# Latent attention on one core: the order of its pieces laid down for TensorE alone, one preparation transpose per q tile, projections further ahead, rotary k scaled by POOL

## The chip, the cores and the metric

The kernel runs on one core of a Trainium2 chip, as one program launch. The metric is device time in microseconds (us), from the start to the end of an execution; lower is better. TensorE (PE in the profile) multiplies matrices, VectorE (DVE), ScalarE (ACT) and GpSimd (POOL) work element by element, and SyncE (SP) issues the transfers between HBM and the core's on-chip memory.

## What is computed

Two layers on a residual stream x of 512 rows by 2048 columns, in float32. Layer A is a gated pooling mixer; then one shared key/value side is made, and layer B is a latent attention of 16 heads. Only the attention matters here; the reference, cut to it:

```python
def chunk_causal_attention(q, k, v):
    S = q.shape[1]
    scale = QK_HEAD ** -0.5
    outs = []
    for i in range(S // QBLOCK):
        q0, k_end = i * QBLOCK, (i + 1) * QBLOCK
        s = jnp.einsum('bqhd,bkhd->bhqk', q[:, q0:k_end], k[:, :k_end]) * scale
        q_chunk = (q0 + jnp.arange(QBLOCK)) // CHUNK
        k_chunk = jnp.arange(k_end) // CHUNK
        s = jnp.where((k_chunk[None, :] <= q_chunk[:, None])[None, None], s, -1e30)
        p = jax.nn.softmax(s, axis=-1).astype(v.dtype)
        outs.append(jnp.einsum('bhqk,bkhd->bqhd', p, v[:, :k_end]))
    return jnp.concatenate(outs, axis=1)

def mla_layer(x, k, v, norm_g, w_in, q_latent_g, w_q_b, q_norm_g, w_out, cos, sin):
    ...
    q = (rmsnorm(q_lat, q_latent_g) @ w_q_b).reshape(B, S, N_HEADS, QK_HEAD)
    q = qk_norm_rope(q, q_norm_g, cos, sin)
    o = chunk_causal_attention(q, k, v).reshape(B, S, W_B)
    return x + (o * jax.nn.silu(gate)) @ w_out
```

k and v of a head come from a latent of 512 columns by `kv_w_b`; k has 128 columns of its own and 64 rotary columns that all heads share, and is normed like q. The kernel computes every product in three passes (high by high, high by low, low by high part), so every operand is split in two: ACT casts the high part, DVE subtracts it to get the low part.

## The kernel before

The program has three stages on TensorE. The first two (layer A and the projections into latents and gates) are dense runs of matmuls up to about 1440 us. The third is the attention with the output projection, up to the end.

**Groups, heads, tiles.** The 16 heads go in 8 groups (`hg`) of two heads (`h`), each head in 4 q tiles (`i`). A group's 8 tiles are numbered 0 to 7 here (4h + i).

**Preparation of a group** (`prep_items`). `kv_part` (L641 to L643) projects k and v of both heads, 4 row tiles of 4 pieces, each piece three matmuls of 512 columns; `q_part` (L664 to L666) does so for q, with 384 columns. A piece reads one of four weights, loaded by SP into `raw`, cast by ACT (L126, `whi`) and subtracted by DVE (L127, `wlo`); four of them are held, and the next is loaded when the weight four before it has had its last use. `kstats_unit` forms the inverse norm of k on DVE: sums of squares from ACT, L684 and L685, a reciprocal square root of three Newton steps (L158 to L163) on tiles of 128x8, and then eight scalings of k in place (L692). `krot_unit` scales the shared rotary k by it, once for each head (L700, on ACT). `qstats_unit` does the same for q, whose factor goes into the exponential; `qrot_unit` (L721 to L724, on POOL) rotates q. At last `tr_unit` transposes what the scores read, through a PSUM bank `tr`: units 0 and 1 are k of the two heads, unit 2 the rotary k of a head (L736), units 3 and 4 q of the two heads, and unit 5 the rotary q (the others at L753). Four TensorE transposes of 128x128 make a unit; ACT and DVE then read the bank to split it.

**A tile of attention.** `score_unit` multiplies q by k (L787, five matmuls of up to 512 columns) into one of two `sc` banks; DVE masks (L788), takes the row maximum (L790) and multiplies it by the norm of q (L792). `exp_unit` lets ACT form the exponential with its sum (L800). `scale_unit` takes the reciprocal (L806) and scales (L807) on DVE. `pt_unit` transposes P on TensorE (L815), through the same two `tr` banks, and splits it (L149, the line of the helper `split`). `pv_unit` multiplies by v (L840 to L842) after every second tile, and at a head's end DVE multiplies by the gate (L845).

**What sets the order.** The main loop walks over the 64 tiles: score of tile m, PV of m-2 where due, exponential of m, transpose of P of m-1, scaling of m. Between these it calls `fill_to`, which takes pieces from one long list, `fill`: the preparation of all groups, two gates, the first parts of the output projection. Each entry has a length in TensorE time, and `base` says how much of the list must be done when a group's first tile begins: up to its last preparation transpose (unit 5) and 2.3 us more (`AHEAD`). At the end the instructions of this stage are chained on TensorE, ACT and DVE, each in the order in which the program wrote them; POOL and SP are left to the scheduler, which orders an engine's instructions by its own plan. TensorE, ACT, DVE and POOL each work through their queue in order, so an instruction that waits holds up all behind it.

Of the kernel before, what the change touches and what calls it, by code (L numbers as in the profile page):

```python
# [10 lines left out]
AF = mybir.ActivationFunctionType  # L11
ALU = mybir.AluOpType
AX = mybir.AxisListType

P = 128
# [25 lines left out]

AHEAD = 2.3


@with_exitstack
def trunk_kernel(
# [17 lines left out]
    V, A, G, T = nc.vector, nc.scalar, nc.gpsimd, nc.tensor  # L66
# [21 lines left out]
    def tt_(n=S, dt=F32):  # L88
        return tp[0].tile([P, n], dt, tag="t", name="tt_")
# [10 lines left out]
    def f(ap):  # L100
        return ap.bitcast(F32)
# [46 lines left out]
    def split(src, hi, lo):  # L148
        return A.copy(hi, src), V.tensor_tensor(lo, src, f(hi), ALU.subtract)  # L149
# [112 lines left out]
    with ExitStack() as c1:  # L262
# [97 lines left out]
        with ExitStack() as c2:  # L360
            hp = c2.enter_context(tc.tile_pool(name="hp", bufs=2, **tile_))
            for j in range(NJ):
# [3 lines left out]
                c = x_load(j)  # L366
                raw = hp.tile([P, 4, 2, P], F32, tag="hraw", name="hraw")
                hi = w7.tile([P, 4, 2, P], F32R, tag="hi", name="hi")
                lo = w7.tile([P, 4, 2, P], F32R, tag="lo", name="lo")
                parts = None  # L370
                for m in (0, 2):
# [3 lines left out]
                    parts = parts or x_parts(j, c, hp)  # L375
# [16 lines left out]
        for o in range(0, 4, 2):  # L392
            e = epool.tile([P, 7, H], F32, tag="e", name="e")
# [72 lines left out]
    for g in range(NG):  # L466
# [11 lines left out]
        for o in range(KD):  # L478
            first = len(wloads)
# [15 lines left out]
    for k in range(KD):  # L495
        hi, lo = at(), at()
# [182 lines left out]
    def kstats_unit(hg):  # L679

        d = st[hg]
        v, a, y = small(8, "sv", 2), small(8, "sa", 2), small(8, "sy", 2)
        for t in range(4):
            V.tensor_scalar(v[:, 2 * t:2 * t + 2], d["ssk"][:, 2 * t:2 * t + 2], kr2[:, t:t + 1], None, ALU.add)  # L684
        V.tensor_scalar(v, v, 1.0 / 192, EPS, ALU.mult, ALU.add)  # L685
        rsqrt(v, y, a, 8)
        d["yk"] = y
        for t in range(4):
            for h in range(2):
                c = 2 * t + h  # L690
                kk = d["kraw"][t // 2][:, t % 2, h * P:(h + 1) * P]
                V.tensor_scalar(kk, kk, y[:, c:c + 1], None, ALU.mult)  # L692

    def krot_unit(hg, h):
        d = st[hg]
        y = d["yk"]
        d.setdefault("krs", []).append(tt_())
        for t in range(4):
            c = 2 * t + h
            A.activation(d["krs"][h][:, t * P:(t + 1) * P].rearrange("p (a d) -> p a d", a=2),  # L700
                         krr[:, t:t + 1, :].broadcast_to([P, 2, 64]), AF.Copy, scale=y[:, c:c + 1])

    def qstats_unit(hg):

# [66 lines left out]
    def score_unit(hg, h, i):  # L771
        d = st[hg]
        n = (i + 1) * P
        if i == 2:

            gt = d[("G", h)] = bt(dt=F32)
            nc.sync.dma_start(gt, gates[2 * hg + h])
        s = sc()
        kh, kl = d[("T", h)]
        krh, krl = d["kr"][h]  # L780
        qh, ql_ = d[("T", 3 + h)]
        qr = d["qr"][h]
# [5 lines left out]
        V.memset(s[0:64, n - 64:n], -1e30)  # L788
        nm = small(1, "nm", 4)
        V.tensor_reduce(nm, s[:, 0:n], AX.X, ALU.max)  # L790
        rq = d["rq"][:, 2 * i + h:2 * i + h + 1]
        V.scalar_tensor_tensor(nm, nm, -1.0, rq, ALU.mult, ALU.mult)  # L792
        d[("P", h, i)] = s, nm, rq
# [9 lines left out]
    def scale_unit(hg, h, i):  # L803
        pe, sm = st[hg][("P", h, i)]
        n = (i + 1) * P
        V.reciprocal(sm, sm)  # L806
        V.tensor_scalar(pe[:, 0:n], pe[:, 0:n], sm, None, ALU.mult)  # L807

    def pt_unit(hg, h, i):

        d = st[hg]
        pe, _ = d.pop(("P", h, i))
        p = tr()
        for j in range(i + 1):
            T.transpose(p[:, j * P:(j + 1) * P], pe[:, j * P:(j + 1) * P], ident)  # L815
# [4 lines left out]
        c = (i % 2) * P  # L820
        for a in range((i + 2) // 2):
            nb = min(2, i + 1 - 2 * a)
            src = p[:, 2 * a * P:(2 * a + nb) * P].rearrange("p (j q) -> p j q", j=nb)
            split(src, d["pth"][a][:, 0:nb, c:c + P], d["ptl"][a][:, 0:nb, c:c + P])

    def pv_unit(hg, h, pr):
        d = st[hg]
# [22 lines left out]
    def prep_items(hg, nxt, mid=()):  # L850


        def piece(us, fn, *a, w=None):
            return us, w, fn, a

        def k(t, i):
            return piece(0.69, kv_part, hg, t, i, w=(wkvb[hg, :, i * 512:(i + 1) * 512], 512))

        def q(t, i):
            return piece(0.53, q_part, hg, t, i, w=(wqb[hg, :, i * 384:(i + 1) * 384], 384))  # L860

# [10 lines left out]
        end = hg == nhg - 1  # L872
        first += mid
        if end:
            first += ld(0, 1, 2, 3)
        first += [q(0, 0), q(0, 1), kq(3), q(0, 2), q(0, 3), piece(0, kstats_unit, hg),
                  q(1, 0), q(1, 1), qq(0), q(1, 2), q(1, 3), kr(0), tr_(0), qq(1), tr_(1),
                  q(2, 0), q(2, 1), kr(1)] + (og(0) if end else []) + [
                  q(2, 2), tr_(2, 0), q(2, 3), tr_(2, 1)] + (og(1) + ld(4, 5) if end else []) + [
                  q(3, 0), qq(2), q(3, 1)] + (og(2) + ld(6, 7) if end else []) + [  # L880
                  q(3, 2), q(3, 3)] + (og(3) if end else [])
        return (first + nxt[:2] + [qq(3), piece(0, qstats_unit, hg), tr_(3)] + nxt[2:3] + [tr_(4)] +
                nxt[3:4] + [tr_(5)] + nxt[4:])


    ogs = [None] * NH
# [121 lines left out]
    base, c = [], 0.0  # L1008
    for t, _, fn, a in fill:
        c += t  # L1010
        if fn is tr_unit and a[1] == 5:
            base.append(c + AHEAD)
    base.append(c)
    SLOT, MAIN = 12.2 / 8, (0.99, 2.0, 1.09, 2.03)
    fill_to(base[0])
    seq = [(hg, h, i) for hg in range(nhg) for h in range(2) for i in range(4)]


    for m in range(len(seq) + 2):
        now = seq[m] if m < len(seq) else None  # L1020
        if now:
            hg, h, i = now
            each = (base[hg + 1] - base[hg]) / 8
            at_ = base[hg] + each * (4 * h + i) + sum(SLOT - MAIN[j] for j in range(i))
            share = each + SLOT - MAIN[i]
            score_unit(*now)
        if m >= 2 and seq[m - 2][2] % 2:
# [92 lines left out]
```

## Time and profile before

| what | us |
|---|---|
| three runs | 2058.01, 2057.32, 2051.13 |
| their median | 2057.32 |
| the profiled execution | 2057.44 |
| its span, first to last instruction | 2055.7 |
| first matmul of the first `kv_part` | 1439.9 |
| first score of group 0 | 1499.82 |
| first score of group 7 | 1863.56 |

The span is the time between the first and the last instruction on the core; the execution's own time is 1.74 us longer. In the slices of the page, each 51.4 us long, the attention fills numbers 30 to 37 of 40. A digit there is the busy share of an engine in tenths; PEclk is the clock that TensorE was granted, in tenths of full speed. In a row of groups the columns are line, engine, operation, output<-inputs, shape and count, then busy us and mean ns, then the idle time ahead of it and what ended it. In a row of waits: who waited for whom, us in total, times, the longest. In the timeline: start, length, instruction, and in brackets the wait before it with what ended it.

### The profile page before, as it was taken

How to read it: one execution, taken by the hardware profiler on the slowest of the kernel's cores; microseconds unless marked ns; L12 is line 12 of the kernel's file. 1: busy time of each engine (PE TensorE's matmuls, PEld its weight loads, DVE VectorE, ACT ScalarE, POOL GpSimd, SP SyncE). 2: the span in 40 equal slices, each digit the busy share in tenths (PEclk: the TensorE clock that was granted, in tenths of full speed). 3: DMA queues.
4: the chain of work that ended last, by engine and by line, in shares of the span. 5: the costliest groups of instructions: out<-in, count | busy, mean ns of one | idle time of the engine just before them, and what ended most of it. 6: DMA issues, size and time to landing. Idle time of an engine off the chain costs nothing. (4 is left out here: it accounts for less than half of the span.)

```text
span 2055.7 us, 30705 instructions
## 1 busy us (share of the span) xinstructions
PE 1961.6 (95%) x11356; PEld 1735.4 (84%) x11356; DVE 1300.5 (63%) x2297; ACT 828.0 (40%) x1570; POOL 253.0 (12%) x404
## 2 busy tenths in 40 slices
PE   8999999999999999999999999999977888888999
PEld 7999999999999778888888888888866777777887
DVE  8677776886666774866845666533466666666432
ACT  7434333333334332333334533322455555554221
POOL 0423333332231000000000000000111111110000
PEclk9999999999999999999999999999989888889999
DMA  5544444344444464344433433334221111222642
GB/s 186 167 154 155 144 134 128 124 140 144 134 148 146 152 199 131 123 138 123 139 118 121 147 97 103 113 118 123 89 67 57 57 57 57 65 89 85 207 123 88
DMA packets 176647, 251.27 MB, mean 122 GB/s; under 512 B 15728, under 2 KB 95984, under 8 KB 176496
## 3 DMA queue, kind: packets, MB, share of 16 engines
q1 hardware_dynamic: 176208, 249.10, 38.6%
q8 instruction: 89, 1.46, 0.3%
q14 instruction: 62, 0.51, 0.1%
q10 hardware_dynamic: 288, 0.20, 0.0%
HBM read 216.21 MB, written 33.03 MB: 121 GB/s over the span
## 5 line engine op out<-in xcount | busy, mean ns | idle before, releaser
L126 ACT CAST whi<-raw 128x512 fp32r<-128x512 f32 (+2 forms) x421 | 254.0, 608 | 521.6 <-PE mm L145 432.4
L333 PE MATMUL k<-xc,hi 128*128 128x256 f32 x1680 | 460.1, 283 | 0.1
L335 PE MATMUL k<-xc,hi 128*128 128x256 f32 x1680 | 460.0, 283 | 0.0
L127 DVE TENSOR_TENSOR wlo<-raw,whi 128x512 fp32r<-128x512 f32 (+2 forms) x421 | 283.1, 674 | 262.3 <-ACT whi L126 258.0
L337 PE MATMUL k<-xc,lo 128*128 128x256 f32 x1680 | 417.9, 283 | 1.4 <-DVE lo L315 1.3
L144 PE MATMUL mm<-bt,whi 128*128 128x512 f32 x944 | 368.2, 390 | 2.8 <-ACT bt L149 2.8
L146 PE MATMUL mm<-bt,wlo 128*128 128x512 f32 x944 | 368.7, 391 | 1.5 <-DVE wlo L127 1.5
L145 PE MATMUL mm<-bt,whi 128*128 128x512 f32 x944 | 367.7, 390 | 0.1
L315 DVE TENSOR_TENSOR lo<-raw,hi 128x1792 fp32r<-128x1792 f32 x120 | 249.0, 2075 | 158.3 <-ACT hi L314 158.2
L314 ACT CAST hi<-raw 128x1792 fp32r<-128x1792 f32 x120 | 202.7, 1689 | 362.9 <-PE k L337 253.3
L333 PEld LDWEIGHTS k<-xc,hi 128*128 128x128 f32 x1680 | 322.5, 192 | 0.4 <-ACT hi L314 0.3
L335 PEld LDWEIGHTS k<-xc,hi 128*128 128x128 f32 x1680 | 322.5, 192 | 0.0
L337 PEld LDWEIGHTS k<-xc,lo 128*128 128x128 f32 x1680 | 296.8, 192 | 2.7 <-DVE lo L315 2.2
L144 PEld LDWEIGHTS mm<-bt,whi 128*128 128x128 f32 x944 | 177.3, 188 | 40.6 <-ACT bt L149 3.7
L146 PEld LDWEIGHTS mm<-bt,wlo 128*128 128x128 f32 x944 | 177.3, 188 | 39.7 <-DVE wlo L127 2.7
L145 PEld LDWEIGHTS mm<-bt,whi 128*128 128x128 f32 x944 | 177.3, 188 | 37.5 <-DVE bt L149 0.9
L146 PE MATMUL mm<-at,wlo 128*128 128x512 f32 x432 | 169.1, 391 | 1.4 <-DVE wlo L127 1.4
L145 PE MATMUL mm<-at,whi 128*128 128x512 f32 x432 | 169.7, 393 | 0.3 <-DVE at L149 0.2
L144 PE MATMUL mm<-at,whi 128*128 128x512 f32 x432 | 169.2, 392 | 0.0
L310 POOL TENSOR_TENSOR raw<-raw 128x256 f32<-128x256 f32 x120 | 98.5, 821 | 439.8 <-DVE raw L308 423.3
L311 POOL TENSOR_TENSOR raw<-raw 128x256 f32<-128x256 f32 x120 | 98.9, 824 | 9.2
L146 PEld LDWEIGHTS mm<-at,wlo 128*128 128x128 f32 x432 | 81.5, 189 | 19.3 <-DVE wlo L127 2.3
(1150 smaller groups left out, 2608.7 us busy)
## 6 DMA issues: line engine op xcount, KB each, us to landing
raw<-awin SPq DMA_DIRECT2D x240, 256.0 KB, 3.2
raw<-awo SPq DMA_DIRECT2D x128, 256.0 KB, 2.8
raw<-bwin SPq DMA_DIRECT2D x80, 256.0 KB, 2.8
raw<-awg SPq DMA_DIRECT2D x64, 256.0 KB, 2.8
raw<-bwo SPq DMA_DIRECT2D x59, 256.0 KB, 2.8
scr<-e SPq DMA_DIRECT2D x56, 256.0 KB, 2.6
raw<-wkvb SPq DMA_DIRECT2D x32, 256.0 KB, 2.9
raw<-wqb SPq DMA_DIRECT2D x32, 192.0 KB, 2.4
```

Of the source, the lines that this page charges most:

```text
L126: A.copy(hi[:, :n], raw[:, :n])
L127: V.tensor_tensor(lo[:, :n], raw[:, :n], f(hi[:, :n]), ALU.subtract)
L144: T.matmul(dst, wh, xh, start=first, stop=False)
L145: T.matmul(dst, wh, xl, start=False, stop=False)
L146: T.matmul(dst, wl, xh, start=False, stop=last)
L310: G.tensor_tensor(c[:, :, 6, :], c[:, :, 4, :], c[:, :, 2, :], ALU.add)
L311: G.tensor_tensor(c[:, :, 7, :], c[:, :, 6, :], c[:, :, 3, :], ALU.add)
L314: A.copy(hi, c[:, :, 1:8, :])
L315: V.tensor_tensor(lo, c[:, :, 1:8, :], f(hi), ALU.subtract)
L333: T.matmul(dst, hi[:, j % 2, wi, :], xh[j][:, xi, :], start=first, stop=False, skip_group_check=True)
L335: T.matmul(dst, hi[:, j % 2, wi, :], xl[j][:, xi, :], start=False, stop=False, skip_group_check=True)
L337: T.matmul(dst, lo[:, j % 2, wi, :], xh[j][:, xi, :], start=False, stop=last, skip_group_check=True)
```

## The change

The diff, cut to its core:

```diff
-AHEAD = 2.3
+AHEAD = 6.5
...
     def kstats_unit(hg):
...
-        for t in range(4):
-            for h in range(2):
-                c = 2 * t + h
-                kk = d["kraw"][t // 2][:, t % 2, h * P:(h + 1) * P]
-                V.tensor_scalar(kk, kk, y[:, c:c + 1], None, ALU.mult)
+        for a in range(2):
+            kk = d["kraw"][a].rearrange("p b (h c) -> p (b h) c", h=2)
+            V.tensor_tensor(kk, kk, y[:, 4 * a:4 * a + 4].unsqueeze(2).broadcast_to([P, 4, P]), ALU.mult)

     def krot_unit(hg, h):
...
-        for t in range(4):
-            c = 2 * t + h
-            A.activation(d["krs"][h][:, t * P:(t + 1) * P].rearrange("p (a d) -> p a d", a=2),
-                         krr[:, t:t + 1, :].broadcast_to([P, 2, 64]), AF.Copy, scale=y[:, c:c + 1])
+        o = tt_()
+        yk = d["yk"].rearrange("p (t h) -> p t h", h=2)[:, :, h:h + 1].broadcast_to([P, 4, 64])
+        ov = o.rearrange("p (t a d) -> p t a d", t=4, a=2)
+        for a in range(2):
+            G.tensor_tensor(ov[:, :, a, :], krr, yk, ALU.mult)
+        d.setdefault("krs", []).append(o)
...
     def pt_unit(hg, h, i):
...
-            split(src, d["pth"][a][:, 0:nb, c:c + P], d["ptl"][a][:, 0:nb, c:c + P])
+        for src, hi, lo in parts:
+            A.copy(hi, src)
+        for src, hi, lo in parts:
+            V.tensor_tensor(lo, src, f(hi), ALU.subtract)
...
-        if fn is tr_unit and a[1] == 5:
+        if fn is q_squares and a[1] == 3:
             base.append(c + AHEAD)
     base.append(c)
-    SLOT, MAIN = 12.2 / 8, (0.99, 2.0, 1.09, 2.03)
+    MAIN = (0.99 + 0.45, 2.0 + 0.45, 1.09 + 0.45, 2.03)
+    SLOT = sum(MAIN) / 4
...
+    side = {(0, 1): [(0, tr_unit, 1)], (1, 1): [(0, tr_unit, 2, 1)], (2, 1): [(0, tr_unit, 4), (1, kstats_unit)],
+            (3, 1): [(1, krot_unit, 0)], (4, 1): [(1, tr_unit, 0), (1, krot_unit, 1)], (5, 1): [(1, tr_unit, 2, 0)],
+            (6, 1): [(1, qstats_unit), (1, tr_unit, 3)], (7, 0): [(1, tr_unit, 5)]}
...
             scale_unit(*now)
+            beside(hg, 4 * h + i, 1)
             fill_to(at_ + share)
     fill_to(c + 99)
+    PINNED = (mybir.EngineType.PE,)
     prev = {}
     for ins in block[begin:]:
         e = ins.engine
-        if e in (mybir.EngineType.PE, mybir.EngineType.Activation, mybir.EngineType.DVE):
+        if e in PINNED:
```

In `side` the key is a tile of the group and the half of the tile; the entries are what is written there, with 0 for the group itself and 1 for the next one. So of a group's seven transposes those of its second head (units 1, 2 and 4) move into its own tiles 0 to 2, and the others into tiles 4 to 7 of the group before; the statistics of k come in tile 2 of the group before, those of q in tile 6. In `prep_items` these pieces leave the list, except in group 0, which keeps units 0, 2 (head 0), 3 and 5 and its statistics there. `base` now counts up to the last squares of q, and 6.5 us more. ACT and DVE are no longer chained. A helper's line stands no longer for the split of P, which the change writes out (L826 and L828), and the lines behind the first edit shift: L752 and L735 are the preparation transposes, L786 the scores, L814 the transpose of P, L787, L789, L791, L805 and L806 the DVE steps of a tile, L690 the scaling of k.

**TensorE, between the last tile of head 0 and the second of head 1, in a middle group.** Names: `tt__` is a scaled tile P, `tr` the bank, `mm` a projection piece, `sc` a score; x8 means eight alike in a row. Before:

```order
L815 MATMUL tr<-cs,tt__16485 128x128 x3
L664 MATMUL mm<-whi,at 128x384
L665 MATMUL mm<-whi,at 128x384
L666 MATMUL mm<-wlo,at 128x384
L753 MATMUL tr<-cs,at 128x128 x8
L787 MATMUL sc<-bt 128x128 x5
```

Now, from the first score of head 1 on (of the four pieces of `mm` around the transposes one is shown):

```order
L786 MATMUL sc<-bt 128x128 x5
L814 MATMUL tr<-cs,tt__16534 128x128 x4
L664 MATMUL mm<-whi,at 128x384
L665 MATMUL mm<-whi,at 128x384
L666 MATMUL mm<-wlo,at 128x384
L752 MATMUL tr<-cs,at 128x128 x4
L786 MATMUL sc<-bt 128x256 x5
```

The two units of k stood back to back ahead of head 1's first score; now one unit stands in head 1's first tile, behind the transpose of P and projection pieces, and the other has moved into the next group.

**DVE, the statistics of k, in a middle group.** `sv`, `sa` and `sy` are the 128x8 tiles of the square root, `kr` the rotary part of the norm, `at` holds k. Before (the second and third Newton step, alike, are left out):

```order
L807 TENSOR_SCALAR tt__16485<-tt__16485,sm 128x384
L684 TENSOR_SCALAR sv<-ssk,kr_12522 128x2 x4
L685 TENSOR_SCALAR sv<-sv 128x8
L158 TENSOR_SCALAR sy<-sv 128x8
L159 TENSOR_SCALAR sv<-sv 128x8
L161 TENSOR_TENSOR sa<-sy 128x8
L162 TENSOR_TENSOR sa<-sa,sv 128x8
L163 SCALAR_TENSOR_TENSOR sy<-sa,sy 128x8
L692 TENSOR_SCALAR at<-at,sy 128x128 x8
L788 MEMSET sc 64x64
L790 TENSOR_REDUCE nm<-sc 128x1
```

Now, from a Newton step on:

```order
L161 TENSOR_TENSOR sa<-sy 128x8
L805 RECIPROCAL sm<-sm 128x1
L162 TENSOR_TENSOR sa<-sa,sv 128x8
L806 TENSOR_SCALAR tt__17011<-tt__17011,sm 128x384
L163 SCALAR_TENSOR_TENSOR sy<-sa,sy 128x8
L765 SCALAR_TENSOR_TENSOR bt<-tr,gqk,bt 128x512
L787 MEMSET sc 64x64
L789 TENSOR_REDUCE nm<-sc 128x1
L791 SCALAR_TENSOR_TENSOR nm<-nm,qy 128x1
L690 TENSOR_TENSOR at<-at,sy 128x512 x2
```

The statistics were one unbroken block ahead of the next tile's mask; now a tile's reciprocal, scaling, mask and maximum lie between their steps.

**DVE, behind the maximum of head 1's second tile.** `nm` is the maximum, `wlo` a weight's low part, `ov` the result of PV. Before:

```order
L788 MEMSET sc 64x64
L790 TENSOR_REDUCE nm<-sc 128x1
L792 SCALAR_TENSOR_TENSOR nm<-nm,qy 128x1
L845 TENSOR_TENSOR bt<-ov,bt 128x512
L127 TENSOR_TENSOR wlo<-raw,whi 128x512 x2
```

Now (a third `wlo`, alike, stands between L849 and L791):

```order
L787 MEMSET sc 64x64
L127 TENSOR_TENSOR wlo<-raw,whi 128x512
L789 TENSOR_REDUCE nm<-sc 128x1
L149 TENSOR_TENSOR bt<-tr,bt 128x512
L849 TENSOR_TENSOR bt<-ov,bt 128x512
L791 SCALAR_TENSOR_TENSOR nm<-nm,qy 128x1
```

The product behind the maximum followed it at once; now an eviction, the gate's product and a weight's low part stand between the two.

More of the change, by code (lines that the diff above doesn't have):

```diff
@@ L820, in pt_unit @@
         c = (i % 2) * P
+        parts = []
         for a in range((i + 2) // 2):
             nb = min(2, i + 1 - 2 * a)
-            src = p[:, 2 * a * P:(2 * a + nb) * P].rearrange("p (j q) -> p j q", j=nb)
-            split(src, d["pth"][a][:, 0:nb, c:c + P], d["ptl"][a][:, 0:nb, c:c + P])
+            parts.append((p[:, 2 * a * P:(2 * a + nb) * P].rearrange("p (j q) -> p j q", j=nb),
+                          d["pth"][a][:, 0:nb, c:c + P], d["ptl"][a][:, 0:nb, c:c + P]))
+        for src, hi, lo in parts:
+            A.copy(hi, src)
+        for src, hi, lo in parts:
+            V.tensor_tensor(lo, src, f(hi), ALU.subtract)
     def pv_unit(hg, h, pr):
@@ L872, in prep_items @@
         end = hg == nhg - 1
+        own = hg == 0
         first += mid
@@ L875, in prep_items @@
             first += ld(0, 1, 2, 3)
[L876 to L883, printed above, removed]
+        first += [q(0, 0), q(0, 1), kq(3), q(0, 2), q(0, 3)]
+        if own:
+            first += [piece(0, kstats_unit, hg)]
+        first += [q(1, 0), q(1, 1), qq(0), q(1, 2), q(1, 3)]
+        if own:
+            first += [kr(0), tr_(0)]
+        first += [q(2, 0), qq(1), q(2, 1)]
+        if own:
+            first += [kr(1)]
+        if end:
+            first += og(0)
+        first += [q(2, 2), q(2, 3)]
+        if own:
+            first += [tr_(2, 0)]
+        if end:
+            first += og(1) + ld(4, 5)
+        first += [q(3, 0), qq(2), q(3, 1)]
+        if end:
+            first += og(2) + ld(6, 7)
+        first += [q(3, 2), q(3, 3)]
+        if end:
+            first += og(3)
+        first += nxt[:1] + [qq(3)]
+        if own:
+            return first + [piece(0, qstats_unit, hg), tr_(3)] + nxt[1:4] + [tr_(5)] + nxt[4:]
+        return first + nxt[1:]
     ogs = [None] * NH
@@ L1010, in trunk_kernel, with beside @@
         c += t
-        if fn is tr_unit and a[1] == 5:
+        if fn is q_squares and a[1] == 3:
             base.append(c + AHEAD)
     base.append(c)
-    SLOT, MAIN = 12.2 / 8, (0.99, 2.0, 1.09, 2.03)
+    MAIN = (0.99 + 0.45, 2.0 + 0.45, 1.09 + 0.45, 2.03)
+    SLOT = sum(MAIN) / 4
     fill_to(base[0])
     seq = [(hg, h, i) for hg in range(nhg) for h in range(2) for i in range(4)]
+    side = {(0, 1): [(0, tr_unit, 1)], (1, 1): [(0, tr_unit, 2, 1)], (2, 1): [(0, tr_unit, 4), (1, kstats_unit)],
+            (3, 1): [(1, krot_unit, 0)], (4, 1): [(1, tr_unit, 0), (1, krot_unit, 1)], (5, 1): [(1, tr_unit, 2, 0)],
+            (6, 1): [(1, qstats_unit), (1, tr_unit, 3)], (7, 0): [(1, tr_unit, 5)]}
+    def beside(hg, n, part):
+        for x, fn, *a in side.get((n, part), ()):
+            if hg + x < nhg:
+                fn(hg + x, *a)
     for m in range(len(seq) + 2):
@@ L1026, in trunk_kernel @@
             score_unit(*now)
+            beside(hg, 4 * h + i, 0)
         if m >= 2 and seq[m - 2][2] % 2:
```

2 lines of the change are left out of this document (removed).

## The prediction

> **What bounds the kernel now.** I read the page first. TensorE is busy nearly all the time except in slices 32 to 37, which are the attention; there the granted clock drops too.
>
> ```profile
> PE 1961.6 (95%) x11356; PEld 1735.4 (84%) x11356; DVE 1300.5 (63%) x2297; ACT 828.0 (40%) x1570; POOL 253.0 (12%) x404
> PE   8999999999999999999999999999977888888999
> PEclk9999999999999999999999999999989888889999
> ```
>
> Then the table by stretches, cut at the first score matmul of a group of two heads (1499.82 us is group 0, 1863.56 group 7; the third row is group 3, typical of the middle). Columns: length, then busy time of PE, PEld, DVE, ACT, POOL, then granted clock.
>
> ```profile
> 1475.00:1499.82 24.82, 20.13 (x88) 16.54 (x88) 15.60 (x51) 14.99 (x47) 6.78 (x16) 0.82 0.21 66
> 1499.82:1863.56 363.74, 294.84 (x1540) 253.63 (x1539) 242.03 (x778) 206.07 (x673) 45.50 (x112) 0.88 0.21 66
> 1654.01:1705.23 51.22, 41.76 (x221) 36.10 (x220) 34.11 (x111) 28.89 (x97) 6.45 (x16) 0.87 0.18 57
> 1863.56:1905.00 41.44, 36.66 (x190) 30.41 (x189) 26.02 (x72) 18.76 (x48) 0.00 (x0) 0.96 0.21 65
> ```
>
> In the seven groups TensorE idles 363.74 - 294.84 = 68.9 us, and the clock takes (1 - 0.88) x 363.74 = 43.6 us more at most (some of the half-speed time falls into the waits). So TensorE's own work at full clock is at least 294.84 - 43.6 = 251.2 us, or 35.1 us in group 3 (41.76 - 0.13 x 51.22), against 51.2 us taken. No other engine is full: DVE 67%, ACT 57%.
>
> Next, whom TensorE waits for in the attention (us in total, times, longest).
>
> ```profile
> PE tr L753 <- DVE xt L149: 19.5, 6, 3.3
> PE tr L753 <- DVE bt L766: 18.5, 7, 2.7
> PE tr L753 <- DVE at L692: 15.8, 7, 2.5
> PE tr L815 <- DVE sc L788: 6.7, 10, 1.8
> PE tr L736 <- DVE xt L149: 5.5, 6, 0.9
> ```
>
> The preparation transposes (L753, L736) carry 19.5 + 18.5 + 15.8 + 5.5 = 59.3 us. The timeline shows how one such pair arises in group 3:
>
> ```profile
> 1669.55 1.12 DVE L684 TENSOR_SCALAR sv<-ssk,kr 128x2 f32<-128x2 f32 x4
> ...
> 1672.93 0.17 DVE L163 SCALAR_TENSOR_TENSOR sy<-sa,sy 128x8 f32<-128x8 f32 x1
> 1673.14 1.66 DVE L692 TENSOR_SCALAR at<-at,sy 128x128 f32<-128x128 f32 x8
> 1673.57 1.41 PE L753 MATMUL tr<-cs,at 128*128 128x128 f32 x4 [2.24 <-DVE at L692]
> 1674.80 0.11 DVE L788 MEMSET sc<- 64x64 f32 x1
> ...
> 1675.86 0.78 ACT L800 ACTIVATE tt__16571<-sc,nm,qy 128x512 f32<-128x512 f32 x1 [5.49 <-DVE nm L792]
> ...
> 1677.03 0.42 DVE L149 TENSOR_TENSOR xt<-tr,xt 128x256 fp32r<-128x256 f32 x1 [1.20 <-ACT xt L149]
> ...
> 1678.22 1.09 PE L753 MATMUL tr<-cs,at 128*128 128x128 f32 x4 [3.24 <-DVE xt L149]
> ```
>
> The k statistics run as one block of 5.2 us on DVE (1669.55 to 1674.80). The transpose of k waits for its end; the finished scores' mask stands behind it, so ACT stands 5.49 us before its exponential; and the second transpose waits for a `tr` bank whose eviction stands behind all that. The clock follows the waits:
>
> ```profile
> 1542.57 1.12 PE L753 MATMUL tr<-cs,qt 128*128 128x128 f32 x4 [2.72 <-DVE bt L766]
> ...
> 1543.91 0.63 PE L642 MATMUL mm<-whi,at 128*128 128x512 f32 x1
> 1544.34 0.63 PE L643 MATMUL mm<-wlo,at 128*128 128x512 f32 x1
> ...
> 1553.02 0.63 PE L815 MATMUL tr<-cs,tt__15154 128*128 128x128 f32 x4 [1.12 <-DVE sc L788]
> ...
> 1553.94 0.40 PE L643 MATMUL mm<-wlo,at 128*128 128x512 f32 x1
> 1554.18 0.40 PE L641 MATMUL mm<-whi,at 128*128 128x512 f32 x1
> ```
>
> After a wait of 2.72 us the 512-wide matmuls follow each other at 0.43 us, after one of 1.12 us at 0.24. The attention is bound by TensorE held up in a few long waits, each of them paid twice.
>
> **The change, part by part.**
>
> *One preparation transpose per q tile.* The pairs and triples that fought over two `tr` banks go; in the new order there is at least a score and a projection piece between two of them, mostly a whole q tile (35.1 / 8 = 4.4 us), and the k statistics are laid down in tile 2 for the transpose in tile 4. The 59.3 us of waits lose their reason, and with them most of the clock's share. What is late next is whatever DVE cannot deliver, since TensorE would need only 35.1 us a group.
>
> *DVE's load.* The eight scalings of k become two of 128x512. Of the operation itself, a product with a broadcast column, no row exists; the nearest is a two-input DVE pass of that size.
>
> ```profile
> L692 DVE TENSOR_SCALAR at<-at,sy 128x128 f32<-128x128 f32 x8 | 1.7, 280 | 0.0
> L149 DVE TENSOR_TENSOR bt<-tr,bt 128x512 fp32r<-128x512 f32 x4 | 2.8, 689 | 1.9 <-ACT bt L149 1.7
> ```
>
> 1.66 us go and 2 x 0.69 = 1.38 come: 0.28 a group less (bounds: half of that row, 0.7 us a group less again, to twice it, 1.4 more). DVE's 242.03 us in the seven groups become 240.1. That is 96% of TensorE's 251.2: the two would be almost equally full, each in a fixed order and each waiting for the other. How full does DVE get while it is the one waited for?
>
> ```profile
> 1669.01:1676.51 7.50, 3.60 (x21) 2.48 (x19) 6.23 (x30) 1.98 (x8) 1.50 (x4) 0.91 0.07 27
> 1671.51:1674.01 2.50, 0.44 (x2) 0.28 (x2) 2.20 (x13) 0.00 (x0) 0.00 (x0) 1.00 0.00 0
> ```
>
> 6.23 / 7.5 = 83% over the block, 2.20 / 2.5 = 88% at its densest; the rest are gaps inside chains and waits for ACT. I take 85% between the two: 240.1 / 0.85 = 282.5 us for the seven groups, a gain of 81.2 us. A group then lasts some 40 us, TensorE waits 5 us in it, 0.6 us a tile, below the 1.12 us that left the clock alone.
>
> *Orders of ACT and DVE no longer chained.* No instruction is added. The split of P now casts both halves before it subtracts, and the statistics' short steps lie between other work in the new DVE order: the 5.2 us block is gone. But the same freedom puts up to three 0.7 us passes between a tile's maximum and the step behind it; that is in the 85% as long as it is not everywhere (rival 4). As a bound: nothing gained by it, or 0.5 us a tile.
>
> *Rotary k on POOL.* ACT loses eight copies a group, POOL gains four products of 128x256.
>
> ```profile
> L700 ACT ACTIVATE tt__16595<-krr,sy 128x128 f32<-128x128 f32 x4 | 1.3, 403 | 0.0
> L310 POOL TENSOR_TENSOR raw<-raw 128x256 f32<-128x256 f32 x120 | 98.5, 821 | 439.8 <-DVE raw L308 423.3
> ```
>
> ACT gets 2 x 1.3 = 2.6 us a group back (two heads), off the path. POOL needs 4 x 0.82 = 3.3 us a group on top of 6.45, so it stays below 30% of 40 us. Each head's pair takes 1.64 us, and the transpose that reads it comes two tiles (8.8 us) after the product for head 0 and five for head 1; only q's rotations stand in POOL's queue with it. Cost nothing on the path; without that cover 1.64 us a head, 23 us in seven groups. That POOL holds DVE up can be seen where they meet:
>
> ```profile
> 1691.39 0.82 DVE L127 TENSOR_TENSOR wlo<-raw,whi 128x512 fp32r<-128x512 f32 x1 [0.61 <-ACT whi L126]
> 1691.62 0.77 POOL L723 TENSOR_TENSOR tt__16506<-qt,qsin 128x64 f32<-128x64 f32 x1
> ```
>
> This DVE pass took 0.13 us more than the 0.69 of a like one. With all four products meeting such a pass, 0.5 us a group: 4 us in the end, which the range holds. The Trainium skill speaks against the move: page GPSIMD Engine Reference, section 1, Specifications, has GpSimd share its SBUF interfaces with VectorE, with contention for DVE instructions of two SBUF inputs. The two rows agree that they contend; rival 3 is its full price.
>
> *Projections run further ahead.* Their matmuls are the same and so are their weights; the loads move with the pieces, four weights ahead as now, past the gate loads in SP's queue.
>
> ```profile
> raw<-wkvb SPq DMA_DIRECT2D x32, 256.0 KB, 2.9
> ```
>
> A load lands in 2.9 us, and no weight is among TensorE's longer waits above. From the last use of a weight to the first use of its successor there are still three pieces (9 matmuls) plus, now, a score and a PV step. Cost 0; 1 us a group if the cover went.
>
> *Ends.* Before group 0 (1475.00 to 1499.82) TensorE idles 4.7 us and loses 0.18 x 24.8 = 4.5 us to the clock; the k statistics there are as close to their transpose as before, the triple at the end is spread: 4 us gained (0 to 9). In group 7 4.8 us of idling and 1.7 us of clock stand against three transposes that move in: 2 us gained (0 to 6).
>
> **Sum.** 81.2 + 4 + 2 = 87 us, made against the profiled execution's 2057.44 us (span 2055.7 plus 1.74 around it), which is 0.1 us from the median of the three runs: **1970 us**.
>
> **Rivals.**
> 1. *TensorE stays the bound.* DVE's new order has fewer waits at its head and fills to 95%; a group costs 35.1 to 37 us. At the floor the seven groups gain 363.74 - 251.2 = 112.5 us, with the ends 118.5: 1939 us. Against it: where TensorE now runs without a stop, DVE is only 9.62 / 15 = 64% busy, so such a pace leaves work behind, which the block of the statistics then shows; for it: no row shows DVE unable to do more.
>
> ```profile
> 1654.01:1669.01 15.00, 15.00 (x85) 13.10 (x84) 9.62 (x30) 9.09 (x38) 0.00 (x0) 1.00 0.29 90
> ```
>
> 2. *The waits are spread, not removed, and the clock goes on halving.* TensorE's 251.2 us at the clock of now are 251.2 / 0.88 = 285.5, and six us of waits a group, moved from L753 to P's transpose and PV, add 42: 327.5, a gain of 36.2 us, none at the ends: 2021 us. For it: waits of 2 to 3 us already halve the clock. Against: the 1.12 us wait kept full speed.
> The Trainium skill, page TensorE: Matmul & The Clock Gate, section A second HAM failure mode: psum-queue depth-cycling, describes such a kernel, whose brief pauses between groups of matmuls made the clock swing. By that rule this rival holds; the one short wait quoted disagrees.
>
> 3. *POOL holds DVE up for as long as it multiplies.* DVE loses 3.3 us a group: (240.1 + 23) / 0.85 = 309.5, a gain of 54 and 6 at the ends: 1997 us. For it: the pair of rows above. Against: there it was 0.13 us, not 0.77.
>
> 4. *Slower.* Place: DVE's queue between a tile's maximum (L790) and its negated product (L792), and from there to the reciprocal (L806). With the order left free, passes of 0.7 us (weight remainders, evictions) get in between.
>
> ```profile
> L790 DVE TENSOR_REDUCE nm<-sc 128x1 f32<-128x512 f32 x2 | 1.4, 691 | 0.1
> L792 DVE SCALAR_TENSOR_TENSOR nm<-nm,qy 128x1 f32<-128x1 f32 x8 | 1.3, 159 | 0.3
> L806 DVE RECIPROCAL sm<-sm 128x1 f32<-128x1 f32 x8 | 1.2, 153 | 0.0
> L807 DVE TENSOR_SCALAR tt__16310<-tt__16310,sm 128x512 f32<-128x512 f32 x1 | 0.5, 486 | 0.0
> ```
>
> The chain of the widest tile is 0.11 + 0.69 + 0.16 + 0.78 (ACT) + 0.15 + 0.49 = 2.4 us; in the new order P's transpose comes some 1.2 tiles (5.3 us) after its score, so 2.9 us of foreign work are free. It decides from 2.9 + (51.2 - 35.1) / 8 = 4.9 us of foreign work in every tile; at 5.4 us a tile waits 2.5 us, a group costs 55.1 us, and 7 x 3.9 = 27 us are lost: 2085 us. For it: in group 3 ACT stands 5.49 us for just this. Against: the new order has such passes there (2.1 us) at one tile of eight.
>
> 5. *No difference*: the freed orders put back what the spreading gains. That the change does not do what it says is excluded by TensorE's new order.
>
> **How the numbers follow.** Forecast (DVE 80 to 88% full, 1961 to 1988 us) 0.48, rival 1 0.18, rival 2 with what lies between it and the forecast 0.18, rival 3 0.04, slower 0.06, no difference 0.06. The range reaches from rival 1's floor to just short of rival 2's end, 1938 to 2016; left out are rivals 4 and 5 and the tail of rival 2. A measurement of this kernel can tell about 0.5% (10 us) from no change: faster 0.48 + 0.18 + 0.18 + 0.04 = 0.88, same 0.06, slower 0.06.
>
> **What would show it.** Right: L753's and L736's waits fall from 59 us to under 10; a middle group takes 38 to 42 us with the clock above 0.95 and DVE at 80 to 88%; the waits left stand at L815's and L840's counterparts, none above 1.5 us. Rival 1: DVE above 90%. Rival 2: groups of 45 us, clock below 0.92. Rival 3: DVE's passes longer by 0.3 us and more beside POOL. Slower: ACT waiting over 4 us for L792's counterpart in most tiles. Wrong altogether: a middle group of 50 us or more.

## The result, and the profile after

The changed kernel took 1938.43 us (median of 4 runs, 1935.33 to 1941.53), the one before 2057.24 us. The ratio is 0.9429, its 95% interval 0.9404 to 0.9453. The time lies 0.4 us inside the lower edge of the predicted range, and two of the four runs lie below it: it is that of rival 1, not of the forecast, and that the range holds it is luck.

The page of the profiled execution (1935.33 us, span 1933.4): the dip in slices 30 to 37 is gone, from TensorE's row and from the clock's.

```profile
PE 1910.7 (99%) x11356; PEld 1704.1 (88%) x11356; DVE 1279.4 (66%) x2249; ACT 806.7 (42%) x1506; POOL 287.3 (15%) x436
PE   8999999999999999999999999999999999999999
PEclk9999999999999999999999999999999999999999
```

The stretches that answer to those of before: the 24.8 us ahead of group 0, the seven groups (first score 1492.18, group 7 at 1743.90), group 3, and 41.4 us from group 7 on. Columns as before: length, busy PE, PEld, DVE, ACT, POOL, then the clock.

```profile
1467.36:1492.18 24.82, 23.33 (x119) 19.86 (x118) 11.06 (x29) 13.70 (x40) 8.44 (x20) 1.00 0.29 86
1492.18:1743.90 251.72, 248.58 (x1534) 225.12 (x1533) 223.73 (x738) 187.32 (x617) 72.86 (x140) 1.00 0.30 94
1597.97:1633.32 35.35, 35.35 (x222) 32.19 (x220) 31.63 (x106) 26.09 (x89) 10.04 (x20) 1.00 0.27 83
1743.90:1785.34 41.44, 38.61 (x216) 33.00 (x215) 27.28 (x77) 19.85 (x51) 0.00 (x0) 1.00 0.28 87
```

The seven groups take 251.72 us where they took 363.74. In group 3 TensorE does not stop at all, and DVE, at 31.63 of 35.35 us, is 89% busy. The span shrank by 122.3 us: 112.0 in the seven groups, 7.6 before them (1499.82 to 1492.18), 2.6 after. This is the fastest of the four runs; by the medians 118.8 us are gained. The stages ahead of the attention, whose code no edit touches, add some noise: the first matmul of `kv_part` comes between 1438.28 and 1443.20 us in the 14 profiled executions of this document.

TensorE's waits from group 0 on, up to 1800 us. The first is in group 7; the other two are all that the seven groups have:

```profile
PE tr L814 <- DVE tt__18804 L806: 2.7, 1, 2.7
PE tr L814 <- DVE tt__18109 L806: 2.4, 1, 2.4
PE tr L814 <- DVE tt__14821 L806: 0.7, 1, 0.7
```

59.3 us of waits at the preparation transposes have become none. Nor does TensorE wait for a weight (L126, L127) in the seven groups, though the projections run further ahead. The timeline shows DVE at the end of k's statistics in group 3, the place where the block of 5.2 us stood:

```profile
1610.01 0.16 DVE L161 TENSOR_TENSOR sa<-sy 128x8 f32<-128x8 f32 x1
1610.08 0.15 DVE L805 RECIPROCAL sm<-sm 128x1 f32<-128x1 f32 x1
1610.20 0.17 DVE L162 TENSOR_TENSOR sa<-sa,sv 128x8 f32<-128x8 f32 x1
1610.28 0.41 DVE L806 TENSOR_SCALAR tt__16443<-tt__16443,sm 128x384 f32<-128x384 f32 x1
...
1612.72 0.11 DVE L787 MEMSET sc<- 64x64 f32 x1 [0.19 <-PE sc L786]
1612.75 0.15 DVE L162 TENSOR_TENSOR sa<-sa,sv 128x8 f32<-128x8 f32 x1
1612.87 0.69 DVE L789 TENSOR_REDUCE nm<-sc 128x1 f32<-128x512 f32 x1
...
1613.67 1.71 DVE L690 TENSOR_TENSOR at<-at,sy 128x512 f32<-128x512 f32 x2
1613.70 0.49 PE L814 MATMUL tr<-cs,tt__16443 128*128 128x128 f32 x3
```

A reciprocal, a scaling, a mask and a maximum pass between the steps of the square root; nobody waits for its end.

### The profile page after: what moved, and what is told of

Read it like the earlier page. It is cut to its first block, busy times and chain, and to the rows that moved or that the text cites. A ratio compares the mean times of both kernels' runs of the same rounds, so it can differ in the third digit from the quotient of the medians.

```text
span 1933.4 us, 30664 instructions
## 1 busy us (share of the span) xinstructions
PE 1910.7 (99%) x11356; PEld 1704.1 (88%) x11356; DVE 1279.4 (66%) x2249; ACT 806.7 (42%) x1506; POOL 287.3 (15%) x436
## 4 chain that ended last, share of the span: by engine, by line
PE 88%; DMA 4%; DVE 4%; issue 1%; ACT 1%; SPq 1%; POOL 0%; DVEq 0%; ACTq 0%; POOLq 0%
PE mm L146 15%; PE mm L144 14%; PE mm L145 14%; PE k L337 10%; PE k L335 10%; PE k L333 10%; PE sc L786 2%; PE mm L641 2%; PE mm L643 1%; PE mm L642 1%; PE mm L664 1%; PE mm L666 1%; PE mm L665 1%; PE tr L814 1%; PE tr L752 1%
## 5 line engine op out<-in xcount | busy, mean ns | idle before, releaser
L126 ACT CAST whi<-raw 128x512 fp32r<-128x512 f32 (+2 forms) x421 | 254.4, 609 | 515.7 <-PE mm L145 444.4
L127 DVE TENSOR_TENSOR wlo<-raw,whi 128x512 fp32r<-128x512 f32 (+2 forms) x421 | 285.0, 678 | 237.7 <-ACT whi L126 236.5
L310 POOL TENSOR_TENSOR raw<-raw 128x256 f32<-128x256 f32 x120 | 97.1, 809 | 434.4 <-DVE raw L308 412.2
L311 POOL TENSOR_TENSOR raw<-raw 128x256 f32<-128x256 f32 x120 | 105.7, 880 | 9.2
```

What stands on the lines that cost most here:

```text
L126: A.copy(hi[:, :n], raw[:, :n])
L127: V.tensor_tensor(lo[:, :n], raw[:, :n], f(hi[:, :n]), ALU.subtract)
L310: G.tensor_tensor(c[:, :, 6, :], c[:, :, 4, :], c[:, :, 2, :], ALU.add)
L311: G.tensor_tensor(c[:, :, 7, :], c[:, :, 6, :], c[:, :, 3, :], ALU.add)
```

## The experiments

All are edits of the changed kernel but the second, which is one of the kernel before. Medians, and ratios to the kernel before with their intervals:

| kernel | us | ratio (95%) |
|---|---|---|
| the change | 1938.43 | 0.9429 (0.9404 to 0.9453) |
| e1 all chained | 2025.26 | 0.9852 (0.9833 to 0.9871) |
| e2 before, only freed | 1990.60 | 0.9683 (0.9665 to 0.9702) |
| e3 rotary k on ACT | 1945.95 | 0.9466 (0.9450 to 0.9481) |
| e4 one more maximum a tile | 1942.39 | 0.9447 (0.9427 to 0.9467) |
| e5 only DVE freed | 1953.50 | 0.9506 (0.9484 to 0.9528) |
| e6 only ACT freed | 1990.77 | 0.9685 (0.9671 to 0.9700) |
| e7 two more maxima a tile | 1956.95 | 0.9523 (0.9509 to 0.9537) |
| e8 old forms of both | 1955.53 | 0.9514 (0.9500 to 0.9529) |
| e9 old split | 1949.89 | 0.9484 (0.9470 to 0.9498) |
| e10 eight scalings | 1943.88 | 0.9458 (0.9442 to 0.9474) |
| e11 half pieces | 1932.65 | 0.9404 (0.9390 to 0.9418) |
| e12 place and freed alone | 1971.03 | 0.9586 (0.9570 to 0.9602) |

### e1: the new places, all three engines chained

```diff
-    PINNED = (mybir.EngineType.PE,)
+    PINNED = (mybir.EngineType.PE, mybir.EngineType.Activation, mybir.EngineType.DVE)
```

> The change with ACT and DVE chained again in the order in which the program writes them; everything else of the change stays. Place theory (the waits came from where the transposes stood in TensorE's order): the long waits stay away, 1935 to 1965 us, middle groups of 35.3 to 38 us. Order theory (they came from DVE's queue, and freeing it did it): the statistics are a block on DVE again and the waits come back at P's transpose, 2000 us or more, middle groups above 44 us. My own guess lies between: about 1965 us, since the block of some 5 us stands ahead of a mask once a group and P's transpose has 2.9 us to spare.

Measured: 2025.26 us. Place theory falls as the whole explanation, and so does my guess of 1965. A middle group, and TensorE's longest waits of the execution:

```profile
1587.87:1635.66 47.79, 39.82 (x222) 35.24 (x221) 34.10 (x105) 26.06 (x89) 10.11 (x20) 0.89 0.20 62
```

```profile
PE tr L814 <- DVE sc L787: 44.7, 13, 4.7
```

The timeline of such a wait:

```profile
1607.55 0.83 DVE L684 TENSOR_SCALAR sv<-ssk,kr 128x2 f32<-128x2 f32 x4
...
1611.17 1.72 DVE L690 TENSOR_TENSOR at<-at,sy 128x512 f32<-128x512 f32 x2
...
1612.89 0.11 DVE L787 MEMSET sc<- 64x64 f32 x1
...
1613.95 0.78 ACT L799 ACTIVATE tt__15966<-sc,nm,qy 128x512 f32<-128x512 f32 x1 [4.69 <-DVE nm L791]
...
1616.01 0.49 DVE L806 TENSOR_SCALAR tt__15966<-tt__15966,sm 128x512 f32<-128x512 f32 x1
...
1616.65 1.09 PE L814 MATMUL tr<-cs,tt__15966 128*128 128x128 f32 x4 [4.39 <-DVE sc L787]
```

With the program's order the statistics are a block again, 1607.55 to 1612.89. The mask stands behind it, the exponential behind the mask, and now P's transpose waits, 4.39 us, where the k transposes had waited. The wait moved; it did not go.

### e2: the kernel before, ACT and DVE freed

```diff
-        if e in (mybir.EngineType.PE, mybir.EngineType.Activation, mybir.EngineType.DVE):
+        if e in (mybir.EngineType.PE,):
```

> The kernel before with ACT and DVE no longer chained, TensorE's order unchanged. Place theory: the pairs and triples of transposes still wait for their two banks, 2030 us or more. Order theory: 1940 to 1980 us.

Measured: 1990.60 us, between the two theories. What is left is a wait at the pair of k transposes, and the timeline shows that it is for the bank: the second unit of transposes starts after the eviction of the `tr` bank by ACT and DVE, with DVE idle ahead of it.

```profile
PE tr L753 <- DVE bt L149: 20.0, 6, 3.4
PE tr L736 <- DVE bt L149: 5.2, 6, 0.9
```

```profile
1596.58 1.42 PE L753 MATMUL tr<-cs,at 128*128 128x128 f32 x4
...
1598.46 1.27 ACT L700 ACTIVATE tt__16063<-krr,sy 128x128 f32<-128x128 f32 x4
1599.63 0.46 ACT L670 COPY qt<-mm 128x384 f32<-128x384 f32 x1
1599.99 0.58 ACT L149 CAST bt<-tr 128x512 fp32r<-128x512 f32 x1
1600.61 0.69 DVE L149 TENSOR_TENSOR bt<-tr,bt 128x512 fp32r<-128x512 f32 x1 [1.88 <-ACT bt L149]
1601.35 1.12 PE L753 MATMUL tr<-cs,at 128*128 128x128 f32 x4 [3.36 <-DVE bt L149]
```

The first unit's transposes end at 1598.00, and ACT casts their bank only at 1599.99: in between it scales the rotary k (L700) and copies a piece (L670). So of the 3.36 us some 2.0 are ACT's order, with work that the change gives to POOL. There were two causes, then, one behind the other: the block in DVE's queue, and the pairs, whose second unit needs a bank that is evicted late. Removing either alone left waits of the other kind. How much the pair would cost with a prompt eviction is not shown.

### e5 and e6: only DVE freed, only ACT freed

```diff
-    PINNED = (mybir.EngineType.PE,)
+    PINNED = (mybir.EngineType.PE, mybir.EngineType.Activation)
```

> The change with ACT chained in the program's order and only DVE (and POOL, SP) left to the scheduler. All chained it took 2025 us, both freed 1938 us. If the block of the statistics in DVE's queue is what chaining costs, freeing DVE alone brings nearly all of it back: 1938 to 1960 us. If ACT's queue is what matters (its casts ahead of the exponential), 2000 us or more.

In e6 the chained engines are TensorE and DVE instead.

> The change with DVE chained in the program's order and only ACT (and POOL, SP) left to the scheduler. If the block of the statistics in DVE's queue is what chaining costs, nothing comes back: 2010 to 2030 us, with the waits at P's transpose as long as with all chained (4.7 us). If ACT's queue matters, 1980 us or less.

Measured: 1953.50 and 1990.77 us. DVE's freedom brings 72 of the 87 us between e1 and the change, as the theory of the block has it. ACT's alone brings 34, which that theory did not foresee. In e6 the same wait is left as in e1, as often and shorter. The seven groups of e1, then of e6:

```profile
PE tr L814 <- DVE sc L787: 42.7, 12, 4.7
PE tr L814 <- DVE sc L787: 26.4, 12, 3.8
```

Freeing ACT lets its casts run where they fit, so DVE enters the block earlier; that this is the way is argued, not shown.

### e4 and e7: how full can DVE get?

```diff
         V.reciprocal(sm, sm)
         V.tensor_scalar(pe[:, 0:n], pe[:, 0:n], sm, None, ALU.mult)
+        for _ in range(2):
+            V.tensor_reduce(small(1, "xm", 2), pe[:, 0:n], AX.X, ALU.max)
```

e4 has the line once, e7 twice.

> The change with one more maximum on DVE in each tile, over the scaled tile, 0.29 to 0.69 us by width, 3.9 us a group, its result unused. DVE is busy 31.6 of 35.35 us in a middle group and would be 35.5. If DVE can be filled to the brim, groups of 35.5 to 36.5 us and 1938 to 1948 us. If it can be filled to 85 to 90% only, as the prediction had it, 35.5 / 0.9 = 39.4 us a group or more: 1965 us and up.

> The change with two more maxima on DVE in each tile, 7.8 us a group, results unused. One of them took a group from 35.35 to 35.84 us with DVE 94% busy. Two ask for about 39 us of DVE in a group, more than TensorE's 35: now DVE is the bound. If it can be filled to 95% and more, groups of 38 to 41 us, 1955 to 1980 us; if not, 43 us or more, 1995 us and up. For the clock: if waits spread thin over the tiles (0.4 to 0.7 us each) leave it alone, it stays at 0.98 or more in the groups; if spread pauses halve it too, it falls below 0.95 and groups cost a further 2 us.

Measured: 1942.39 and 1956.95 us. A middle group of e4, then of e7, then TensorE's waits in that group of e7:

```profile
1601.04:1636.88 35.84, 35.64 (x222) 32.09 (x220) 33.54 (x114) 26.20 (x89) 10.10 (x20) 1.00 0.26 82
```

```profile
1607.45:1645.44 37.99, 35.72 (x221) 32.08 (x220) 36.52 (x122) 26.80 (x89) 10.47 (x20) 1.00 0.26 77
```

```profile
PE tr L816 <- DVE tt__16642 L806: 1.6, 1, 1.6
PE tr L816 <- DVE sm L805: 0.7, 1, 0.7
```

DVE is 33.54 / 35.84 = 94% busy in e4, with TensorE still at work 99% of the time, and 36.52 / 37.99 = 96% in e7. The 85% of the prediction was no limit. The maxima added 1.9 and 4.9 us of busy time, not 3.9 and 7.8, mostly since busy time counts a moment once in which two instructions overlap. And the clock stayed at 1.00 in this group, with 2.3 us of waits, the longest 1.6 us. In e7's group 0 it did not: after waits of 1.42 and 0.52 us at a preparation transpose (1514.52 and 1515.45) the matmuls of 384 columns follow each other at 0.32 us instead of 0.17.

### e3, e8, e9, e10: the forms

e3 puts the rotary k on ACT again (`krot_unit` as before).

> The change with the rotary k scaled on ACT again. If TensorE is the bound with room on ACT (26.1 of 35.35 us busy in a middle group, 28.7 with the copies), no difference: 1933 to 1945 us. If POOL's products cost DVE time that matters, a few us faster than the change; if ACT was close to its limit, 1950 us or more.

Measured: 1945.95 us, 7.5 us more than the change: outside what was expected under the first case, if by little, and the opposite of the second. TensorE waits a little and often, for evictions that ACT begins:

```profile
PE tr L735 <- DVE bt L149: 3.1, 7, 0.5
PE ov L845 <- DVE xt L828: 2.2, 5, 0.4
```

POOL's products do cost DVE time: DVE is busy 30.84 us in group 3 of e3 (1602.72 to 1639.56), against 31.63. Of the changed kernel, the scaling of k (16 times, shortest, median, longest in ns) and two of POOL's pairs; then the scaling in e3, where POOL has no product beside it:

```profile
L690 DVE TENSOR_TENSOR at<-at,sy x16: 684/807/1106, 1459.3 to 1724.3; 128x512 f32<-128x512 f32 x16
```

```profile
L699 POOL TENSOR_TENSOR tt__14440<-krr,sy x2: 612/612/613, 1478.6 to 1479.1; 128x256 f32<-128x256 f32 x2
L699 POOL TENSOR_TENSOR tt__16562<-krr,sy x2: 1057/1058/1059, 1613.8 to 1614.8; 128x256 f32<-128x256 f32 x2
```

```profile
L690 DVE TENSOR_TENSOR at<-at,sy x16: 681/686/692, 1463.0 to 1734.6; 128x512 f32<-128x512 f32 x16
```

The pair at 1613.8 runs beside the scaling of the timeline above (1613.67) and takes 1.06 us a product, against 0.61 undisturbed. Of the two scalings the first keeps its 0.69 us and the second takes 1.11; the median of 0.81 lies between the two kinds. Together they take 1.71 us, against 1.29 in e3:

```profile
1581.63 1.29 DVE L690 TENSOR_TENSOR at<-at,sy 128x512 f32<-128x512 f32 x2
```

The Trainium skill, page GPSIMD Engine Reference, section 1, Specifications, has the two share their SBUF interfaces; these rows agree, and both sides pay.

e8 undoes two forms, the two scalings and P's split:

```diff
-        for src, hi, lo in parts:
-            A.copy(hi, src)
-        for src, hi, lo in parts:
-            V.tensor_tensor(lo, src, f(hi), ALU.subtract)
+            split(src, d["pth"][a][:, 0:nb, c:c + P], d["ptl"][a][:, 0:nb, c:c + P])
...
-        for a in range(2):
-            kk = d["kraw"][a].rearrange("p b (h c) -> p (b h) c", h=2)
-            V.tensor_tensor(kk, kk, y[:, 4 * a:4 * a + 4].unsqueeze(2).broadcast_to([P, 4, P]), ALU.mult)
+        for t in range(4):
+            for h in range(2):
+                c = 2 * t + h
+                kk = d["kraw"][t // 2][:, t % 2, h * P:(h + 1) * P]
+                V.tensor_scalar(kk, kk, y[:, c:c + 1], None, ALU.mult)
```

> The change with the eight scalings of k instead of two, and with P's split as cast and subtraction by turns in the program (the scheduler may order them). If only the places of the transposes, the freed orders and, a little, POOL carry the gain, no difference: 1933 to 1945 us. If the two forms matter for DVE, 1950 us or more.

Measured: 1955.53 us, 17 us more than the change: the second of the two cases. e9 has only the first half of that edit, e10 only the second.

> The change with only P's split written as before, cast and subtraction by turns. With this and the eight scalings it took 1955.5 us, against 1938 us. If the split carries it (PV waited for it there, 3.4 us in all, and P's transpose 1.4 us a group for a scaling), 1950 to 1957 us; if the scalings do, 1936 to 1942 us.

> The change with only the eight scalings of k back. If the scalings carry the 17 us (eight passes of DVE where two were), 1950 to 1957 us; if P's split does, 1936 to 1942 us. Half and half is possible: both near 1947 us.

Measured: 1949.89 and 1943.88 us, 11.5 and 5.5 us more than the change: by the medians together the 17. The intervals of e10's ratio and, by a hair, of e3's overlap that of the change, so the middle groups decide, which are alike within 0.1 us in each of these runs: 35.35 us in the change, 36.45 in e10, 36.84 in e3, 37.43 in e9, 37.64 in e8. So each form is worth something, and in the middle groups the two of e8 hide one another in part (2.3 us, singly 1.1 and 2.1). In e9 PV now waits, once a group, for the second half of P's split:

```profile
PE ov L840 <- DVE xt L149: 7.6, 8, 1.2
```

### e12: places and freed orders without the forms

The forms of e8, and the rotary k on ACT as in e3.

> Only the new places of the transposes and statistics and the freed orders: eight scalings, P's split by turns, and the rotary k on ACT, as before. Undone one at a time these cost 5.5, 11.5 and 7.5 us. If they add up, 1938 + 24.5 = about 1963 us. If they hide one another (all three ask for the same slack of DVE and ACT), about 1950 us; if they worsen one another, 1975 us or more.

Measured: 1971.03 us. The three forms together are worth 32.6 us, 8 more than undone singly. A middle group:

```profile
1609.38:1649.94 40.56, 38.18 (x222) 33.64 (x220) 33.03 (x112) 28.49 (x97) 6.47 (x16) 0.96 0.24 72
```

The clock is at 0.96 again, and TensorE waits no longer than 1.5 us at once:

```profile
1635.44 0.38 PE L841 MATMUL ov<-xt,at 128*128 128x256 f32 x1 [1.48 <-ACT xt L149]
1636.05 0.42 PE L842 MATMUL ov<-xt,at 128*128 128x256 f32 x1 [0.23 <-DVE xt L149]
...
1637.55 0.63 PE L642 MATMUL mm<-whi,at 128*128 128x512 f32 x1
1637.98 0.63 PE L643 MATMUL mm<-wlo,at 128*128 128x512 f32 x1
```

After two short waits close together the 512-wide matmuls follow each other at 0.43 us, as they did before the change after 2.72. The middle group before this one, with no such slow stretch, takes 39.00 us instead of 40.56.

### e11: the last groups' pieces cut in two

```diff
-        return [(0.69 * n, (bwo[o, :, k0 * P:(k0 + n) * P], n * P), out_part, (o, k0, n))]
+        return [(1.38, (bwo[o, :, k0 * P:(k0 + n) * P], n * P), out_part, (o, k0, n, j0)) for j0 in range(0, n, 2)]
```

with `out_part` doing two of a weight's blocks at a time.

> The change with the output projection's pieces between the last tiles cut in two, six matmuls each instead of twelve, so that each of the last two groups' tiles gets one. TensorE is the bound but for waits of 2.4 and 2.7 us at P's transposes in the groups that share their tiles with these pieces, where a tile has no piece. If that theory holds, the two waits go: 4 to 6 us less than the change, about 1933 us. If something else is late at these places (DVE's queue), nothing is gained.

Measured: 1932.65 us (1932.16 to 1935.14), the lowest median of all. It beats the kernel before clearly; against the change it is 5.8 us less by the medians of two different sets of runs, and the intervals of the two ratios overlap by a little. The longest waits at P's transposes in the last two groups:

```profile
PE tr L814 <- DVE nm L791: 2.3, 1, 2.3
PE tr L814 <- DVE tt__18804 L806: 0.5, 1, 0.5
```

The wait of 2.7 us in group 7 went down to 0.5. That of 2.4 in group 6 went, but another of 2.3 came in the same group, at a later tile (1732.23, `tt__18332`), and the group takes 42.21 us instead of 39.77. From the first matmul of `kv_part` to the end the two profiled executions take 492.53 (the change) and 492.27 us (e11): nearly all that lies between their times, 1935.33 and 1932.46, comes from the stages ahead, which the edit does not touch. So these traces show no gain, and whether the 5.8 us are more than noise stays open.

## Why the prediction was right and wrong

**Right: what bound the kernel.** TensorE's own work in the seven groups was put at 251.2 us or more; with the waits gone they take 251.72, of which TensorE is busy 248.58. The bound was 2.6 us too high, and the 3.1 us of idling that are left make up for it. The waits named, 59.3 us at the preparation transposes, are gone, and the clock is back at 1.00. That each wait was paid twice holds as well: of the 112.0 us, 65.8 are idling that went (68.9 to 3.1) and 46.3 busy time that the clock had stretched (294.84 to 248.58). One sign failed: no wait left was to be above 1.5 us, and two are, 2.4 and 2.7.

**Wrong: the step "I take 85% between the two".** It turned the forecast into a DVE that can never be fuller than where it had been the one waited for, and made a group 40 us. A group takes 35.35 us, with DVE at 89%; e4 and e7 filled it to 94 and 96%. The 83 and 88% were read inside the block of the statistics, from a chain whose steps wait for one another: a property of that chain, not of the engine. Rival 1 had this case, floor and time (1939 us), at 0.18. The argument against it was that DVE is only 64% busy where TensorE runs without a stop, so that work must be left behind; the change shows a group in which TensorE never stops and DVE is 89% busy. That rival 1's time agrees within 0.5 us is in part luck: in the profiled execution 122.3 us went, where it had 118.5, and the median lies 3.1 us above that execution.

**Wrong by a mis-sized term: DVE's load.** 0.28 us a group less was predicted, and 34.11 became 31.63: 2.48 less. e1 runs the same instructions in the program's order and takes 34.10, so the forms saved next to nothing there, and 2.47 us come from the order alone. The scaling's own term was mis-sized: two passes were put at 1.38 us against 1.66 for eight, and beside POOL they take 1.71. The instructions did not get shorter by the order: added up one by one, those of the two groups last 36.7 us in e1 and 37.1 in the change, but 2.6 and 4.8 us of that overlap (the change has one pass of 0.7 us at the edge, counted whole). The timeline after shows how: L805 starts at 1610.08 while L161 (1610.01, 0.16 long) still runs, and L162 follows L161 at a distance of 0.19 us with other work in between. Steps that don't depend on one another overlap; in the block before, each step of the root follows the one it depends on at 0.20 us, with nothing between (from the trace: 1671.93, 1672.13, 1672.33, each 0.17 long).

**Half right: where the gain would come from.** The prediction gave the places of the transposes the 59 us and treated the freed orders as a help that could as well be nothing. The runs give: places with the forms, chained (e1), 31 us; freed orders alone (e2) 66; places and freed orders without the forms (e12) 85; everything 119. So e1's and e2's edits together bring 22 us more than singly. That this is because two causes stood one behind the other fits the waits, but it is not shown: the forms, worth 33 us in the end, are in e1 and not in e2, and the places alone were not run. Nor were the greater `AHEAD` and the new pace of the tiles undone; every run with the new places has them.

**Wrong: the forms' terms.** The rotary k on POOL was to "cost nothing on the path", the scalings to bring 2 us in all, and P's split had no price. With TensorE at 100% and DVE at 89%, they are worth 7.5, 5.5 and 11.5 us when undone. In the kernel before, with 9.5 us of idling a group, they might have hidden; that is argued, and no run has them there. The prediction priced them against the old slack instead of the new.

**The ends.** 4 and 2 us were predicted, 7.6 and 2.6 measured, both with the clock at 1.00. Counted from the first matmul of `kv_part`, group 0's first score comes 8.6 us earlier (59.93 to 51.32).

**The other rivals.** Rival 2 (the clock goes on halving): not in the change's profiled execution. The Trainium skill, page TensorE: Matmul & The Clock Gate, section A second HAM failure mode: psum-queue depth-cycling, tells of brief pauses that swing the clock. In kind e12 agrees, with half speed after waits of 1.48 and 0.23 us; the middle group of e7, with single waits of 1.59 and 0.69 us, does not. Rival 3 (POOL holds DVE): real in kind, 0.8 us of DVE's time in a group instead of 3.3, and the move still gains 7.5 us. Rival 4 (slower): freeing the orders was the largest single gain.

## What to carry to other kernels

When two waits may stand one behind the other, price each by what is late next once the other is gone: here the places with the forms gave 31 us, the freed orders 66, both together 119. An engine's busy share inside a dependent chain did not tell how full it can get; to learn that, add load to it and watch the engine that should be the bound. Price a small edit against the slack that will be left after the change, not against that of now.

## What the runs showed of the hardware that I had not expected

- DVE's busy time for the same instructions depends on their order: 34.10 us a group chained (e1), 31.63 with independent steps between dependent ones.
- A POOL product of 128x256 takes 0.61 us undisturbed and 1.06 beside DVE passes with two inputs; of two such passes of 128x512 behind one another the first keeps 0.69 us and the second takes 1.11.
- The length of a wait alone did not decide whether the granted clock halves. At the same transpose of P in group 6 the change's wait of 2.40 us left it at 1.00 (1716 to 1728 us), and e3's of 2.24 (1725 to 1737 us) and e10's of 2.44 (1720 to 1732 us) came with 0.86. A single wait of 1.59 us in e7 left it at 1.00, and 1.48 with 0.23 shortly behind came with 0.96 in the group (e12). Waits of 4.4 us came with 0.89 (e1).
